# Scores of the 64-feature heads in a two-layer hybrid attention block: three products on half of the rows each, two heads side by side

## The chip, the core and the metric

The kernel runs on one core of one Trainium2 chip. The metric is the device time of one execution in microseconds (us): the median of the runs shown. A core has a matrix engine (TensorE, PE in the profile; PEld is its weight loading, which may overlap the products), a vector engine (DVE), a scalar engine (ACT), GpSimd (POOL), and a queue (SP) that issues the transfers. Products read SBUF, which has 128 partitions (called rows here), and write PSUM banks of 128 x 512 floats.

## The reference

Two layers run over 512 latent tokens and 256 context tokens of width 1024. In each layer one input projection feeds three groups of attention heads, whose outputs go through one output projection, and an MLP of width 4096 follows. Groups A (8 query heads, 2 key heads, a window of 128 with sinks) and B (4 heads, a 2-D neighbourhood with a bias) have 64 features in a head, and the change is about their scores alone:

```python
qa = axial_rope(split_heads(xa_q, A_HEADS), row, col)
ka = axial_rope(split_heads(xa_k, A_KV_HEADS), row, col)
out_a = windowed_gqa(qa, ka, split_heads(xa_v, A_KV_HEADS), ka_c, va_c, attn_sink[l])
out_b = neighbourhood_attention(split_heads(xb_q, B_HEADS), split_heads(xb_k, B_HEADS),
                                split_heads(xb_v, B_HEADS), kb_c, vb_c, na_rpb[l])
# inside both: scores over the local keys and over the 256 context keys, one softmax over both
s_loc = jnp.einsum('bnqkgd,bnskd->bnkgqs', qb, kb) * scale
s_ctx = jnp.einsum('bnqkgd,bckd->bnkgqc', qb, k_ctx) * scale
```

Group C (4 latent heads with 64 + 32 features) is not touched. In the first layer the context tokens attend too, so queries cover 768 tokens there and 512 in the second layer.

## The kernel before

Everything is float32. To keep that precision the kernel splits each operand of a product into a high part that the fast format `float32r` holds and a low part, the rest, and computes high x high + low x high + high x low: three products in place of one. All engines' orders are set by a scheduler at build time, which interleaves independent work; nothing in the kernel text fixes where a product stands among its neighbours.

For each layer the order of the text is: a pair of B heads is projected (`proj_B`), attended (`att_B`), then the second pair, then the keys, values and queries of A (`proj_AK`, `proj_AQ`), the attention of half of A's heads (`att_A`), an output-projection part (`w_out_part`), the rest of A, then group C and the MLP.

A projection (`feat_chunk`, L480 to L482, tile `psd`) gives 128 feature rows: two heads of 64, one on rows 0 to 63 and one on rows 64 to 127. It is copied to `qkraw` (`evac_raw`). Then, for each of the two heads, the kernel lays out operands that fill all 128 rows:

- `stack_q` (L556, L557) writes a page `qs` for each head: the high part of q on the head's own rows, the low part on the other 64 rows.
- `dup_k` (L567 to L576) writes pages `kh` and `kl` for each head: the high part of k on both halves of the rows (the second copy is a transfer inside SBUF, L569), and the low part on both halves (the second copy on DVE, L576).

With them `att_unit` (L617) needs two products of 128 rows for a score: `qs` x `kh` sums high x high and low x high, and `qs` x `kl` adds high x low (and low x low). It works on four "rows" at a time: two heads and two blocks of 128 queries (B), or four heads and one block (A). A row has one or two segments: 256 context keys, and 256 or 384 local keys. A segment has one PSUM bank of the three named `pss`; the vector engine takes it out with the mask and the running minimum (L621 without, L628 with a mask; the scores carry a minus sign), ACT makes the exponentials (L633), DVE, POOL or ACT norms them, TensorE turns the probabilities (L668, tile `pst`) and multiplies them with the values (L682, tile `psv`; two heads side by side on 64 columns each). Group C's scores also run at L617, as three products on 96 rows (tiles `kc`, `qc`).

The pages `qs kh kl vtok bias oth otl` come from one ring of 18 buffers (tag `pg`); `oth` and `otl` hold the attention outputs for the output projection. The weights of a projection arrive in one transfer of 128 columns into a ring of four buffers (`raw`).

One other place matters below: L314 in `ada_dve`, in the MLP of the first layer, turns a small tile with TensorE; in some calls the tile has 64 rows only.

Of the kernel before, what the change touches and what calls it, by code (L numbers as in the profile page):

```python
# [44 lines left out]
        "up": 4, "u": 16, "wf": 16, "of": 8, "fg": 2, "ga": 4}  # L45
# [3 lines left out]
for _tag, _names in (  # L49
# [10 lines left out]
    ("pg", "qs kh kl vtok bias oth otl"),  # L60
# [8 lines left out]
    ("ga", "gate"),  # L69
    ("ac", "acc"),  # L70
# [10 lines left out]
def hybrid_dit_kernel(  # L81
# [13 lines left out]
    def bc(ap):  # L95
        return ap.bitcast(F32)

    def sbuf(n, dt, name):
        tag = TAGS[name]
        size = 768 if tag in PAD else 512 if tag in PAD5 else -(-n // 256) * 256  # L100
        return sb.tile([P, size], dt, tag=tag, name=name, bufs=CAPS[tag])[:, :n]

    def page(n, dt=F32, name="pgf"):
        return sbuf(n, dt, name)

# [445 lines left out]
    def stack_q(t_, n):  # L551

        outs = []
        for own, oth in ((H0, H1), (H1, H0)):
            q_ = page(n, F32R, "qs")
            A.copy(q_[own], t_[own])  # L556
            V.tensor_tensor(q_[oth], t_[own], bc(q_[own]), ALU.subtract)  # L557
            outs.append(q_)
        return outs

    def dup_k(t_, n):

        outs = []
        for own, oth in ((H0, H1), (H1, H0)):
            kh = page(n, F32R, "kh")
            kl = page(n, F32R, "kl")
            A.copy(kh[own], t_[own])  # L567
            if DUPDMA & 1:
                nc.sync.dma_start(bc(kh[oth]), bc(kh[own]))  # L569
            else:  # L570
                A.copy(kh[oth], t_[own])
            V.tensor_tensor(kl[own], t_[own], bc(kh[own]), ALU.subtract)
            if DUPDMA & 2:
                nc.sync.dma_start(bc(kl[oth]), bc(kl[own]))
            else:
                V.tensor_copy(kl[oth], bc(kl[own]))  # L576
            outs.append((kh, kl))
        return outs
# [19 lines left out]
    def att_unit(kind, rows, vap, put, sinkcols=None):  # L598


        pts = []
        for r, row in enumerate(rows):
            w_ = sum(s[1] for s in row["segs"])
            we = w_
            init = HUGE
# [6 lines left out]
            off = 0  # L612
            for c0, n, mask in row["segs"]:
                ps = ps_s()
                np_ = len(row["passes"])
                for j, (lh, rh) in enumerate(row["passes"]):
                    T.matmul(ps[:, :n], lh, rh[:, c0:c0 + n], start=(j == 0), stop=(j == np_ - 1))  # L617
                dst = p_[:, off:off + n]
                acc = small(1, "m", 16)
                if mask is None:  # L620
                    V.tensor_scalar(dst, ps[:, :n], 0.0, init, ALU.add, ALU.min, accum_out=acc)  # L621
                else:
                    src = ps[:, :n]
                    if len(mask.shape) == 3:
                        nb = mask.shape[1]
                        src = src.rearrange("p (b c) -> p b c", b=nb)
                        dst = dst.rearrange("p (b c) -> p b c", b=nb)
                    V.tensor_tensor_reduce(out=dst, in0=src, in1=mask, scale=1.0, scalar=init,  # L628
                                           op0=ALU.add, op1=ALU.min, accum_out=acc)
                init = acc  # L630
                off += n
            sm = small(1, "sm", 16)
            A.activation(p_, p_, AF.Exp, scale=-1.0, bias=init, accum_out=sm)  # L633
            V.reciprocal(sm, sm)  # L634
            e_ = NORM[kind][r]
            if e_ == "V":
                V.tensor_scalar(p_[:, :w_], p_[:, :w_], sm, None, ALU.mult)
            elif e_ == "A":
                A.activation(p_[:, :w_], p_[:, :w_], AF.Copy, scale=sm)
            else:  # L640
                G.tensor_tensor(p_[:, :w_], p_[:, :w_], sm.to_broadcast([P, w_]), ALU.mult)  # L641
            pts.append(p_)
# [99 lines left out]
    for l in range(DEPTH):  # L742
# [11 lines left out]
        def new_ot(c):  # L754
            OT[c] = (page(nq, F32R, "oth"), page(nq, F32R, "otl"))
# [4 lines left out]
        def proj_B(p_):  # L760
# [5 lines left out]
            KB[2 * p_], KB[2 * p_ + 1] = dup_k(t_, 768)  # L766
# [4 lines left out]
            QB[2 * p_], QB[2 * p_ + 1] = stack_q(t_, nq)  # L771
# [4 lines left out]
        def att_B(p_):  # L776
# [13 lines left out]
            for u in range(2 if last else 3):  # L790
                rows = []
                for i in range(2):
                    for n in (2 * u, 2 * u + 1):
                        q_ = QB[2 * p_ + i][:, n * P:(n + 1) * P]
                        kh, kl = KB[2 * p_ + i]
# [10 lines left out]
                        rows.append(dict(passes=[(q_, kh), (q_, kl)], segs=segs))  # L806
# [16 lines left out]
        def proj_AK():  # L823
# [3 lines left out]
            KA.extend(dup_k(t_, 768))  # L827
# [6 lines left out]
        def proj_AQ(jp):  # L834
            for c in (jp, jp + 2):
                res = feat_chunk(l, h, c * P, nq)
                t_ = evac_raw(res, -0.125, False)
                rope(t_, ALLP, (rA[:, 0, :], rA[:, 1, :]), SHUF16)
                QA[2 * c], QA[2 * c + 1] = stack_q(t_, nq)
                pump(1)  # L840
# [476 lines left out]
```

## Time and profile before

| what | value |
| --- | --- |
| median of 3 runs | 1644.02 us (1641.97 to 1644.7) |
| profiled execution, its own time | 1647.55 us |
| its span, first to last instruction | 1645.8 us |
| PE busy | 1594.6 us (97%), 8994 instructions |
| DVE / ACT / POOL busy | 1009.0 / 682.6 / 608.3 us |
| granted TensorE clock, mean | 0.995 of the full 2.4 GHz |
| attention of A and B, first layer | about 60 to 330 us |
| attention of A and B, second layer | about 1000 to 1200 us |

A busy PE is not a PE at its peak: products are pipelined, so the duration of one product (0.28 to 0.39 us here) is longer than the distance from its start to the next one's start, which is what a product costs when they follow each other. The distances are read from the starts in the timeline. In the timeline the form `128*128 128x512` means that weights of 128 rows and 128 columns are in the array and 512 columns are moved through; `64*128` is an array used on 64 rows, `128*64` on 64 columns. Instructions of the same line and tiles that follow each other are printed as one row with their count.

### The profile page before, as it was taken

The numbers are of one execution on the slowest core, as the hardware profiler recorded it, in microseconds if no ns is written. First come the engines' busy times: TensorE is split into PE (matmuls) and PEld (weight loads), VectorE is DVE, ScalarE is ACT, GpSimd is POOL, SyncE is SP. The second block draws the span as 40 slices with busy tenths as digits, with TensorE's granted clock in tenths as the row PEclk, the third lists the DMA queues.
The fourth block names the chain that finished last, engine by engine and source line by source line (L and its number), as shares of the span: only waits on it lengthen the run. The fifth ranks groups of instructions, "written<-read, shape, count | busy, mean of one in ns | idle before, by whom it ended". The sixth has DMA issues, their size and how long they took to land.

```text
span 1645.8 us, 24134 instructions
## 1 busy us (share of the span) xinstructions
PE 1594.6 (97%) x8994; PEld 1361.1 (83%) x8994; DVE 1009.0 (61%) x1995; ACT 682.6 (41%) x1342; POOL 608.3 (37%) x564
## 2 busy tenths in 40 slices
PE   5999999999999999999999999999999999999997
PEld 3888789787898988989989779888777788888886
DVE  3565766687887556454445776786687644334445
ACT  4554466665631312212223145446755522223332
POOL 1111643553433353341533341153453333333335
PEclk9999999999999999999999999999999999999999
DMA  9654311230154333334333722211120233333331
GB/s 318 184 154 127 121 51 28 67 78 1 53 168 132 116 109 115 106 93 136 88 108 99 253 68 76 69 53 51 46 80 14 78 93 98 91 103 103 90 106 73
DMA packets 156421, 164.46 MB, mean 100 GB/s; under 512 B 8960, under 2 KB 111368, under 8 KB 156304
## 3 DMA queue, kind: packets, MB, share of 16 engines
q1 hardware_dynamic: 156304, 162.92, 32.8%
q8 instruction: 71, 1.16, 0.3%
q14 instruction: 46, 0.38, 0.1%
HBM read 155.53 MB, written 2.12 MB: 96 GB/s over the span
## 4 chain that ended last, share of the span: by engine, by line
PE 85%; DVE 7%; DMA 4%; issue 2%; ACT 2%; POOL 0%; SPq 0%; POOLq 0%; DVEq 0%; ACTq 0%
PE psd L1102 8%; PE psd L1103 8%; PE psd L1104 8%; PE pss L617 5%; PE psv L682 5%; PE pst L668 4%; PE psd L480 3%; PE psd L482 3%; PE psd L481 3%; PE pss L1138 3%; PE pss L1136 3%; PE pss L1137 3%; PE psd L720 2%; PE psd L722 2%; PE psd L721 2%
## 5 line engine op out<-in xcount | busy, mean ns | idle before, releaser
L739 POOL TENSOR_TENSOR xlat<-xlat,rtmp 128x512 f32<-128x512 f32 x159 | 235.8, 1506 | 272.3 <-DVE rtmp L738 269.5
L464 DVE TENSOR_TENSOR wl<-raw,wh 128x1024 fp32r<-128x1024 f32 (+1 forms) x168 | 219.0, 1304 | 184.1 <-issue 82.0
L463 ACT CAST wh<-raw 128x1024 fp32r<-128x1024 f32 (+1 forms) x168 | 174.5, 1039 | 297.6 <-PE pst L1138 179.6
L1102 PE MATMUL psd<-hT,wh 128*128 128x384 f32 (+2 forms) x752 | 264.9, 353 | 3.4 <-DVE hT L427 3.4
L1103 PE MATMUL psd<-hT,wl 128*128 128x384 f32 (+2 forms) x752 | 264.3, 351 | 2.3 <-DVE wl L464 2.3
L1104 PE MATMUL psd<-hT,wh 128*128 128x384 f32 (+2 forms) x752 | 265.9, 354 | 0.0
L641 POOL TENSOR_TENSOR prob<-prob,sm 128x512 f32<-128x512 f32 (+3 forms) x110 | 127.6, 1169 | 265.4 <-DVE sm L634 225.1
L1111 POOL TENSOR_TENSOR relu<-relu 128x384 f32<-128x384 f32 (+1 forms) x96 | 96.6, 1008 | 316.6 <-ACT uh L1110 292.4
L1109 ACT ACTIVATE relu<-psd 128x384 f32<-128x384 f32 (+1 forms) x93 | 49.1, 528 | 280.5 <-PE psd L1104 278.1
L633 ACT ACTIVATE prob<-prob,m 128x513 f32<-128x513 f32 (+6 forms) x160 | 120.9, 756 | 100.6 <-DVE m L628 69.0
L1102 PEld LDWEIGHTS psd<-hT,wh 128*128 128x128 f32 x752 | 141.5, 188 | 14.3 <-issue 4.1
L1112 DVE TENSOR_TENSOR ul<-relu,uh 128x384 fp32r<-128x384 f32 (+1 forms) x96 | 60.4, 630 | 150.7 <-POOL relu L1111 150.7
L1103 PEld LDWEIGHTS psd<-hT,wl 128*128 128x128 f32 x752 | 141.5, 188 | 12.5 <-DVE wl L464 3.0
L1104 PEld LDWEIGHTS psd<-hT,wh 128*128 128x128 f32 x752 | 141.5, 188 | 12.3 <-issue 2.5
L287 DVE SCALAR_TENSOR_TENSOR acc<-araw,consts,acc 128x512 f32<-128x512 f32 x140 | 117.7, 867 | 6.6 <-DMA araw<-in_w_ada_dram 5.8
L668 PE MATMUL pst<-consts,prob 128*128 128x128 f32 x688 | 106.1, 277 | 2.2 <-POOL prob L641 1.8
L668 PEld LDWEIGHTS pst<-consts,prob 128*128 128x128 f32 x688 | 79.6, 140 | 29.0 <-issue 17.8
L482 PE MATMUL psd<-hT,wl 128*128 128x384 f32 (+1 forms) x280 | 97.7, 349 | 1.1 <-DVE wl L464 1.1
L480 PE MATMUL psd<-hT,wh 128*128 128x384 f32 (+1 forms) x280 | 97.8, 349 | 0.0
L481 PE MATMUL psd<-hT,wh 128*128 128x384 f32 (+1 forms) x280 | 96.6, 345 | 0.0
L1138 PE MATMUL pss<-wh,ul 128*128 128x512 f32 x224 | 87.3, 390 | 0.0
L1137 PE MATMUL pss<-wl,uh 128*128 128x512 f32 x224 | 87.2, 390 | 0.0
(265 smaller groups left out, 3539.6 us busy)
## 6 DMA issues: line engine op xcount, KB each, us to landing
raw<-in_w_mlp_in_dram SPq DMA_DIRECT2D x64, 512.0 KB
raw<-in_w_mlp_out_dram SPq DMA_DIRECT2D x64, 512.0 KB
araw<-in_w_ada_dram SPq DMA_DIRECT2D x112, 256.0 KB
raw<-in_w_in_dram SPq DMA_DIRECT2D x24, 512.0 KB
raw<-in_w_ada_dram SPq DMA_DIRECT2D x24, 512.0 KB
raw<-in_w_ada_dram SPq DMA_DIRECT2D x32, 256.0 KB
raw<-in_w_out_dram SPq DMA_DIRECT2D x8, 512.0 KB
raw<-in_w_out_dram SPq DMA_DIRECT2D x16, 256.0 KB
```

Source lines behind the costliest of these rows:

```text
L463: A.copy(hi, raw)
L464: V.tensor_tensor(lo, raw, bc(hi), ALU.subtract)
L480: T.matmul(ps[:, :n], wh[:, k, :], hh[k][:, s0:s0 + n], start=(k == 0), stop=False)
L481: T.matmul(ps[:, :n], wh[:, k, :], hl[k][:, s0:s0 + n], start=False, stop=False)
L482: T.matmul(ps[:, :n], wl[:, k, :], hh[k][:, s0:s0 + n], start=False, stop=(k == KC - 1))
L668: T.transpose(pt[:, r * P:(r + 1) * P], pts[r][:, pos[r][kb]:pos[r][kb] + P], ident)
L739: (V if fast and (RLAST if fast == "end" and t == 3 else RFAST)[dh] == "V" else G).tensor_tensor(xt[t][:, cs], xt[t][:, cs], tmp, ALU.add)
L1102: T.matmul(o_, wh[:, k, :], hh[k][:, sl], start=(k == 0), stop=False)
L1103: T.matmul(o_, wl[:, k, :], hh[k][:, sl], start=False, stop=False)
L1104: T.matmul(o_, wh[:, k, :], hl[k][:, sl], start=False, stop=(k == KC - 1))
L1137: T.matmul(a_, uh[:, ts_], wl[:, c % 2, :], start=False, stop=False)
L1138: T.matmul(a_, ul[:, ts_], wh[:, c % 2, :], start=False, stop=fin)
```

## The change

- `stack_q` and `dup_k` go. One function `hi_lo` splits a page of two heads in place: high part on ACT, low part on DVE, each on all 128 rows in one instruction. The pages are `qh`, `ql`, `kh`, `kl`, one of each for two heads. The transfers `kh<-kh` and the copies of `kl` go.
- A score is now three products, `qh` x `kh`, `qh` x `kl`, `ql` x `kh`, each on the 64 rows of its head. Two heads that lie on different halves are written in turn, product by product, into two `pss` banks. The built program gives each of these products a tile of 64 rows and 128 columns, at row 0 or at row 64; before, these products had the full tile of 128 by 128, as have all projections, output projections, turnings and the 96-row products of C.
- The reading of a segment moves into a function `evac_seg` and comes after the products of both heads.
- A query chunk of A now joins head c of the first key group with head c of the second, so its weights come in two transfers of 64 columns (`feat_chunk` takes a pair of columns).
- The output pages leave the ring `pg` for one of their own, `ot`, of 8 double pages.

```diff
-    ("pg", "qs kh kl vtok bias oth otl"),
+    ("pg", "qh ql kh kl vtok bias"),
+    ("ot", "ot"),
...
     def feat_chunk(l, h, c0, ntok):
         hh, hl = h
-        wh, wl = load_split([(ALLP, w3(l, c0, P, 0, KC))], [KC, P], {1280: "w3", 1152: "w4"}.get(c0) if l == 0 else None)
+        src = [(ALLP, w3(l, c0, P, 0, KC))] if isinstance(c0, int) else [
+            ((ALLP, ALLP, slice(64 * i, 64 * i + 64)), w3(l, c_, 64, 0, KC)) for i, c_ in enumerate(c0)]
+        wh, wl = load_split(src, [KC, P], {1280: "w3", 1152: "w4"}.get(c0) if l == 0 else None)
...
-    def stack_q(t_, n):
...
-    def dup_k(t_, n):
...
+    def hi_lo(t_, n, name):
+
+        hi, lo = page(n, F32R, name + "h"), page(n, F32R, name + "l")
+        A.copy(hi, t_)
+        V.tensor_tensor(lo, t_, bc(hi), ALU.subtract)
+        return hi, lo
...
+        pts = [None] * 4
+
+        for rs in ([(0, 2), (1, 3)] if "halves" in rows[0] else [(r,) for r in range(4)]):
+            ps_of = {}
+            if len(rs) == 2:
+                for c0, n, _ in rows[rs[0]]["segs"]:
+                    pss = [ps_s() for _ in rs]
+                    for j in range(3):
+                        for r, ps in zip(rs, pss):
+                            lh, rh = rows[r]["halves"][j]
+                            T.matmul(ps[:, :n], lh, rh[:, c0:c0 + n], start=(j == 0), stop=(j == 2))
+                    for r, ps in zip(rs, pss):
+                        ps_of[r, c0] = ps
+                    for r in rs:
+                        evac_seg(r, rows[r], c0, pts, ps_of, sinkcols)
...
-                        q_ = QB[2 * p_ + i][:, n * P:(n + 1) * P]
-                        kh, kl = KB[2 * p_ + i]
+                        hv = (H0, H1)[i]
+                        (qh, ql), (kh, kl) = [[t_[hv] for t_ in q_] for q_ in (QB[p_], KB[p_])]
+                        qh, ql = qh[:, n * P:(n + 1) * P], ql[:, n * P:(n + 1) * P]
...
-                        rows.append(dict(passes=[(q_, kh), (q_, kl)], segs=segs))
+                        rows.append(dict(halves=[(qh, kh), (qh, kl), (ql, kh)], segs=segs))
...
-            for c in (jp, jp + 2):
-                res = feat_chunk(l, h, c * P, nq)
+            for c in (2 * jp, 2 * jp + 1):
+
+                res = feat_chunk(l, h, (c * 64, 256 + c * 64), nq)
...
-                    q_ = QA[hd][:, n * P:(n + 1) * P]
-                    kh, kl = KA[i // 2]
+                    hv = (H0, H1)[hd // 4]
+                    (qh, ql), (kh, kl) = [[t_[hv] for t_ in q_] for q_ in (QA[hd % 4], KA)]
```

The scheduler places the new products anew. On PE at the first attention unit of the first layer (`hT`, `wh`, `wl` are the operands of a projection; L617 is the score before, L585 turns the values) the order before is:

```order
L482 MATMUL psd<-hT_131,wl 128x384
L617 MATMUL pss<-kh,qs 128x256
L617 MATMUL pss<-kl,qs 128x256
L617 MATMUL pss<-kh,qs 128x256
L617 MATMUL pss<-kl,qs 128x256
L617 MATMUL pss<-kh,qs 128x256
L617 MATMUL pss<-kl,qs 128x256
L585 MATMUL psd<-consts,qkraw 128x128 x6
L617 MATMUL pss<-kh,qs 128x384
L617 MATMUL pss<-kl,qs 128x384
L480 MATMUL psd<-hT_117,wh 128x384
```

The same place of the changed program, with the buffers' numbers (`pss_739` and `pss_740` are the two heads of one pair, `pss_753` and `pss_754` those of the next; L629 is the score, L570 turns the values):

```order
L629 MATMUL pss_739<-kh_640,qh_648 128x256
L629 MATMUL pss_740<-kh_640,qh_648 128x256
L629 MATMUL pss_739<-kl_641,qh_648 128x256
L629 MATMUL pss_740<-kl_641,qh_648 128x256
L629 MATMUL pss_739<-kh_640,ql_649 128x256
L629 MATMUL pss_740<-kh_640,ql_649 128x256
L629 MATMUL pss_753<-kh_640,qh_648 128x256
L629 MATMUL pss_753<-kl_641,qh_648 128x256
L629 MATMUL pss_753<-kh_640,ql_649 128x256
L570 MATMUL psd_714<-consts_66,qkraw_709 128x128 x4
L570 MATMUL psd_720<-consts_66,qkraw_709 128x128 x2
L629 MATMUL pss_754<-kh_640,qh_648 128x256
```

The first pair stands in turn; of the second pair one head's three products follow it, and the other head's three come only after the six turnings of L570, since the ring `pss` has three banks. On PE near the end of A in the second layer (L894 to L896 before, L910 to L912 after, are group C's input projection; L668 and L681 turn probabilities) the order before is:

```order
L894 MATMUL psd<-wh,hT_9466 128x416
L617 MATMUL pss<-kh,qs 128x384
L617 MATMUL pss<-kl,qs 128x384
L895 MATMUL psd<-wl,hT_9466 128x416
L682 MATMUL psv<-pT_ring,vtok 64x256 x8
L668 MATMUL pst<-consts,prob 128x128 x8
```

and in the changed program:

```order
L681 MATMUL pst<-consts,prob 128x128 x6
L629 MATMUL pss<-kh,qh 128x384
L629 MATMUL pss<-kl,qh 128x384
L629 MATMUL pss<-kh,ql 128x384
L910 MATMUL psd<-wh,hT_9541 128x416
L911 MATMUL psd<-wl,hT_9541 128x416
L629 MATMUL pss<-kh,qh 128x256
L629 MATMUL pss<-kl,qh 128x256
L629 MATMUL pss<-kh,ql 128x256
```

Here the three products of one head stand alone between full-tile work, in both programs in small groups among other products. Over the whole program the 432 score products of A and B become 648, which stand in 135 unbroken runs. Outside the two attention stretches the order on PE is the same in both programs.

## Rows read from the trace of the kernel before

**Rows 1.** The page: busy us (share), xinstructions; the chain that ended last.

```profile
PE 1594.6 (97%) x8994; PEld 1361.1 (83%) x8994; DVE 1009.0 (61%) x1995; ACT 682.6 (41%) x1342; POOL 608.3 (37%) x564
...
PE 85%; DVE 7%; DMA 4%; issue 2%; ACT 2%; POOL 0%; SPq 0%; POOLq 0%; DVEq 0%; ACTq 0%
```

**Rows 2.** Stretches: length, busy PE, PEld, DVE, ACT, POOL; clock; DMA share; GB/s.

```profile
60.00:330.00 270.00, 266.38 (x1796) 224.94 (x1796) 176.28 (x511) 146.41 (x344) 95.73 (x126) 1.00 0.34 101
330.00:430.00 100.00, 95.31 (x571) 75.93 (x569) 84.74 (x201) 63.54 (x138) 46.17 (x37) 0.98 0.19 48
1000.00:1200.00 200.00, 196.73 (x1251) 168.54 (x1251) 143.93 (x397) 113.88 (x254) 71.71 (x84) 1.00 0.22 63
1200.00:1290.00 90.00, 82.69 (x497) 65.28 (x496) 74.33 (x167) 55.12 (x109) 40.46 (x32) 0.96 0.25 68
```

**Rows 3.** Two waits of PE, 60 to 330 us: total, times, longest.

```profile
PE psa L222 <- DMA raw<-in_w_ada_dram: 1.2, 1, 1.2
...
PE psd L482 <- DVE wl L464: 0.3, 1, 0.3
```

**Rows 4.** Timeline of PE near 1180 us: start, duration, line, tiles, form.

```profile
1180.15 0.28 PE L617 MATMUL pss<-kl,qs 128*128 128x256 f32 x1
1180.27 0.28 PE L617 MATMUL pss<-kh,qs 128*128 128x256 f32 x1
1180.38 0.28 PE L617 MATMUL pss<-kl,qs 128*128 128x256 f32 x1
1180.50 0.27 PE L668 MATMUL pst<-consts,prob 128*128 128x128 f32 x1
```

**Rows 5.** Timeline of PE near 878 us: 64 rows, then the full tile.

```profile
878.25 0.46 PE L314 MATMUL psd<-consts,arow 64*128 64x64 f32 x4 [0.55 <-DVE arow L311]
878.63 0.44 PE L1102 MATMUL psd<-hT,wh 128*128 128x384 f32 x1
878.91 0.33 PE L1103 MATMUL psd<-hT,wl 128*128 128x384 f32 x1
879.08 0.34 PE L1104 MATMUL psd<-hT,wh 128*128 128x384 f32 x1
```

**Rows 6.** Timeline of PE near 940 us, around two turnings on 64 rows.

```profile
939.88 0.39 PE L1165 MATMUL pss<-wfl,uh 128*128 128x512 f32 x1
940.11 0.39 PE L1166 MATMUL pss<-wfh,ul 128*128 128x512 f32 x1
940.42 0.34 PE L314 MATMUL psd<-consts,arow 64*128 64x64 f32 x2
940.69 0.50 PE L1164 MATMUL pss<-wfh,uh 128*128 128x512 f32 x1
941.03 0.39 PE L1165 MATMUL pss<-wfl,uh 128*128 128x512 f32 x1
```

**Rows 7.** Split of k: line, durations min/median/max in ns, shapes.

```profile
L567 ACT CAST kh<-qkraw x12: 827/831/842, 61.6 to 1073.1; 64x768 fp32r<-64x768 f32 x12
L572 DVE TENSOR_TENSOR kl<-qkraw,kh x12: 937/953/956, 62.5 to 1074.3; 64x768 fp32r<-64x768 f32 x12
L576 DVE CAST kl<-kl x12: 543/554/557, 64.5 to 1076.2; 64x768 fp32r<-64x768 f32 x12
```

**Rows 8.** Timeline of PE near 186 us: modulation, tiles of 32 columns.

```profile
185.94 1.07 PE L222 MATMUL psa<-raw,consts 128*32 128x256 f32 x16
```

**Rows 9.** Timeline of PE's weight loads near 940 us.

```profile
939.88 0.19 PEld L1166 LDWEIGHTS pss<-wfh,ul 128*128 128x128 f32 x1
940.42 0.20 PEld L314 LDWEIGHTS psd<-consts,arow 64*128 64x128 f32 x2 [0.35 <-issue]
```

**Rows 10.** Line L314, 870 to 980 us: durations min/median/max in ns.

```profile
L314 PE MATMUL psd<-consts,arow x8: 220/223/272, 878.2 to 974.9; 64*128 64x64 f32 x8
```

**Rows 11.** Timeline of PE near 366 us: turnings, group C's products.

```profile
365.75 1.04 PE L668 MATMUL pst<-consts,prob 128*128 128x128 f32 x8
366.54 0.60 PE L617 MATMUL pss<-kc,qc 96*128 96x256 f32 x3
```

More of the change, by code (lines that the diff above doesn't have):

```diff
@@ L596, in evac_copy, with evac_seg @@
             V.tensor_copy(dst, src)
[L598 to L605, printed above, removed]
+    def evac_seg(r, row, c0, pts, ps_of, sinkcols):
+        w_ = sum(s[1] for s in row["segs"])
+        off = 0
+        for c_, n, mask in row["segs"]:
+            if c_ == c0:
+                break
+            off += n
+        if off == 0:
+            we, init = w_, HUGE
             if sinkcols is not None:
@@ L632, in att_unit @@
[L632 to L641, printed above, removed]
@@ new lines, in evac_seg, with att_unit @@
+        pts[r] = (p_, acc, w_)
+    def att_unit(kind, rows, vap, put, sinkcols=None):
+        pts = [None] * 4
[12 more added lines that the diff above has]
+                        evac_seg(r, rows[r], c0, pts, ps_of, sinkcols)
+            else:
+                row = rows[rs[0]]
+                for c0, n, _ in row["segs"]:
+                    ps = ps_s()
+                    np_ = len(row["passes"])
+                    for j, (lh, rh) in enumerate(row["passes"]):
+                        T.matmul(ps[:, :n], lh, rh[:, c0:c0 + n], start=(j == 0), stop=(j == np_ - 1))
+                    ps_of[rs[0], c0] = ps
+                    evac_seg(rs[0], row, c0, pts, ps_of, sinkcols)
+            for r in rs:
+                p_, init, w_ = pts[r]
+                sm = small(1, "sm", 16)
+                A.activation(p_, p_, AF.Exp, scale=-1.0, bias=init, accum_out=sm)
+                V.reciprocal(sm, sm)
+                e_ = NORM[kind][r]
+                if e_ == "V":
+                    V.tensor_scalar(p_[:, :w_], p_[:, :w_], sm, None, ALU.mult)
+                elif e_ == "A":
+                    A.activation(p_[:, :w_], p_[:, :w_], AF.Copy, scale=sm)
+                else:
+                    G.tensor_tensor(p_[:, :w_], p_[:, :w_], sm.to_broadcast([P, w_]), ALU.mult)
+                pts[r] = p_
@@ L754, in new_ot @@
         def new_ot(c):
-            OT[c] = (page(nq, F32R, "oth"), page(nq, F32R, "otl"))
+            OT[c] = page2(nq, "ot")
         QB, KB, VB = {}, {}, {}
@@ L856, in att_A @@
                         segs.append((b0 * P, (b1 - b0 + 1) * P, maskA[:, m0:m0 + b1 - b0 + 1, :]))
-                    rows.append(dict(passes=[(q_, kh), (q_, kl)], segs=segs))
+                    rows.append(dict(halves=[(qh, kh), (qh, kl), (ql, kh)], segs=segs))
                 def put(pv, n=n, jp=jp):
```

74 lines of the change are left out of this document (25 added, 49 removed).

## Prediction

> **What bounds the kernel now.** I read the page first, for the share of each engine, then the busy time by stretch, the waits of PE in the stretches that the change touches, and last the timeline of PE at single products. The page shows a PE that is busy 97% of the span, and a chain of work that is PE for 85% of it [rows 1]; no other engine is above 61%. A busy PE could still be loosely packed, so the stretches matter more: where A and B are attended, PE is idle for 270 - 266.4 = 3.6 us in the first layer and 200 - 196.7 = 3.3 us in the second, at the full granted clock [rows 2]. One wait in the first of them, for a transfer of the modulation's weights, is 1.2 us of it [rows 3]. So there is almost nothing to win here from DVE, ACT or transfers, and a change in what PE must do goes into the time one for one, less at most these 7 us.
>
> **What a score product costs now.** Starts tell it: L617 starts at 1180.15, 1180.27, 1180.38 and the next work at 1180.50 [rows 4], so a product of 256 columns costs 0.12 us. Products of 384 columns stand 0.17 apart (878.91 to 879.08) [rows 5], those of 512 columns 0.23 (939.88 to 940.11) [rows 6]. That is 256, 384 and 512 columns at 2.4 per ns and 13 ns more, so I use 0.119 and 0.173. The full tile of 128 rows is common to the scores and to all that stands around them, turnings and projections alike, so nothing is paid for passing from one to the other.
>
> **What the change takes away beside PE.** The split of q and k halves its instructions, and their duration hangs on the elements in a row, not on the rows. ACT loses 6 of 12 `kh` of 0.83 us and 12 of 24 `qs` of the same kind, at most as long, 15 us; DVE loses 6 `kl` of 0.95, 12 copies of 0.55 and 12 `qs`, again at most 0.95, some 24 us; 12 transfers inside SBUF go [rows 7]. All this lies beside PE's work. It can give back only PE's idle time, 7 us in the two stretches [rows 2], and not all of that, since a part waits for transfers. I take 3 us; the ends are 0 and 7. The 8 weight loads of A's queries become 16 transfers of half the size; PE waited 0.3 us for weights of a projection [rows 3], the ring of four buffers being ahead, so I take nothing. If that cover failed, each could cost as much as the longest wait on a transfer in the stretch, 1.2 us, some 10 us. The new ring for the outputs only loosens waits; the same 7 us bound it.
>
> **What PE's products cost after.** Before there are 336 products of 256 columns and 96 of 384: 336 x 0.119 + 96 x 0.173 = 56.6 us. Afterwards there are 504 and 144, which one after another would take 84.9 us (+28.3). If every product ran beside its partner on the other half, it would be half, 42.4 us (-14.2). The built order decides between these. In it two products on different halves stand next to each other, free to overlap, less often than the kernel text has them: going through the 135 runs, with a product waiting only for the one before it on its own half, 134 products (105 of 256 columns, 29 of 384) begin while the other half still works. 399 x 0.119 + 115 x 0.173 = 67.4 us remain, **+10.8 us**. That two products on different rows do overlap is not in the trace. The nearest row is that of the modulation's products, which sit on different columns, 32 each: 16 of 256 columns are through in 1.07 us [rows 8], where 256 columns at 2.4 per ns one after another make 1.7; so parts of the array do work side by side. I take overlap, and keep +28.3 as the other end.
>
> **What the change of tile costs.** This is the largest term, and the diff doesn't show it. The trace before has 64-row tiles in three places, L314. Around 940 us the last 512-column product starts at 940.11; the next in the same tile would start at 940.34. The 64-row one starts at 940.42 [rows 6], **0.09 us** late, and its weights are loaded only then, after 0.35 us in which the loader waited for nothing but its turn [rows 9]; a 512-column neighbour's weights are loaded during the product before it. Its second product follows more slowly than the others of its kind: 272 ns against a median of 223 [rows 10], 0.05 us, since the load was not hidden. Way back: the second L314 starts at 940.42 + 0.34 - 0.22 = 940.54 and L1164 at 940.69, 0.15 later; four of the kind at 878 us take 0.46 together [rows 5], which without the last one's 0.22 and the first one's 0.05 leaves 0.06 for each step; again 0.09. And that first full product takes 0.50 instead of 0.39, and the next starts 0.34 after it instead of 0.23 [rows 6]: 0.11 for a load that nothing hid. At 878 us it is the same, 0.28 to the next instead of 0.17 [rows 5].
>
> So a way in and out of the 64-row tile costs 0.09 + 0.11 going in (a load of 128 columns is exposed, as in L1164) and 0.09 + 0.11 coming out, or 0.09 + 0.05 where turnings follow. The built order has 135 runs of new products: 132 are entered from full tiles (3 from another narrow tile, where a change was due anyway), 99 end before full products, 30 before turnings, 6 before value products, which change the tile in any case. 132 x 0.20 + 99 x 0.20 + 30 x 0.14 = 26.4 + 19.8 + 4.2 = **50 us**. Before, the scores cost no change at all. The other narrow tiles change about as often as before. A run that starts where PE waited anyway hides its way in, but there are only 7 us of such waiting.
>
> The Trainium skill, TensorEngine Tiling (Array Packing), Key Properties, says that a change of tiling mode, not merely of the tile, drains TensorE. The trace agrees with 0.09 us each way. The page gives no price; it is the rule that speaks against this change; without a drain the sum would be that of rival (c) below.
>
> **The sum.** 10.8 + 50 - 3 = +58 us on the profiled execution's 1647.55, so 1705.5; it stands 3.5 us above the median of the runs, which makes 1702. Readers of banks are late next: no run of the new order holds more than three segments, the number of `pss` banks, but 27 runs hold all three and need them free at once. I take nothing, as full products stand between; half a microsecond (one reading by DVE) for each would be 13 us.
>
> **The rivals.**
> (a) *Halves do not overlap*: loads of 128 columns for both halves go one after the other, and the weights set the pace. For it: nothing in the trace runs on two row halves at once. Then the products cost +28.3: 1702 + 17.5 = 1720.
> (b) *Half of the tile changes are hidden*: the scheduler often puts a run where PE would have waited, or the load is pulled ahead within the engine. Against it: both places of L314 read above show the whole price. 1702 - 25 = 1677.
> (c) *The other side, not slower*: 64 rows change no tile for PE, as the 96-row products of group C, on the full tile, change none: after eight turnings from 365.75 the first of them starts at 366.54, 0.02 after the last turning [rows 11]. Place: the 132 ways in and out; price nothing instead of 0.38 us a run. Then 10.8 remain, the freed DVE and ACT take back all of the 7 us, and the output pages' own ring takes some of the 4.7 + 7.3 us that PE idles in C's stretches [rows 2]: 1644, no change. It decides from below 0.03 us for a run. The rows of the 64-row tiles speak against it [rows 5, 6, 9].
> (d) *The pairs give their full half and the tile is free*: -14.2 us, 1630. The order doesn't have the pairs, so this is what the change says but not what the program does. The Trainium skill, the same page, Theoretical Speedup, has up to 2x for products of at most 64 rows; no run here shows it yet.
>
> **How the numbers follow.** Chances: forecast 0.60 (1690 to 1715), (a) 0.19, (b) 0.10, (c) 0.06, (d) 0.02, and 0.03 for longer still by waits for banks. The likeliest is 1702. The range that leaves out 2 in 10 goes from (b), 1676, past (a) with a few us of bank waits, to 1726. A measurement of this kernel can tell 0.2%, 3.3 us, from no change. Slower by more than that are the forecast, (a), (b) and the longer case, 0.92; (c) gives 0.05 to no change and 0.01 to faster; (d) makes faster 0.03.
>
> **What would show it.** In the profile after: the stretches outside attention keep their length, and the first stretch grows by some 32 us, the second by some 26 (the first has 74 of the 135 runs and 60 of the 108 pairs of segments). A score's first product starts about 0.09 us later than its neighbour's pace allows, its load begins with it, with 0.3 us or so of idle loader before, and the first product behind a run is 0.11 us longer. Two products on different halves start some 7 ns apart if they overlap, 0.12 if (a) holds. DVE's busy time falls by some 24 us at most, ACT's by 15, and PE's own waits do not grow. The prediction is wrong if the first product of a run starts at the ordinary distance with its weights loaded ahead, or if the time is lost in waits of PE for `pss` banks or weights.

## The result

The changed kernel takes **1692.21 us** (median of 4 runs, 1691.42 to 1693.04) against 1644.17 for the kernel before beside it: **1.0285 times as long**, 95% interval 1.0263 to 1.0307. That is slower by 48 us; forecast were 1702 and a range of 1676 to 1726. The profiled execution has a span of 1690.5 us, 44.7 longer than before.

The page of the changed kernel (busy us and share of the span, then the chain that ended last), against [rows 1]:

```profile
PE 1649.5 (98%) x9210; PEld 1366.1 (81%) x9210; DVE 990.9 (59%) x1965; ACT 671.4 (40%) x1324; POOL 609.5 (36%) x564
...
PE 88%; DVE 6%; DMA 3%; issue 2%; ACT 1%; SPq 0%; POOL 0%; POOLq 0%; DVEq 0%; ACTq 0%
```

PE is busy 54.9 us longer; the other engines have less to do or the same. PE's idle time, span less busy, fell from 51.2 to 41.0 us. Two attention stretches of the changed kernel (length, busy PE, PEld, DVE, ACT, POOL, clock, DMA share, GB/s), against [rows 2]:

```profile
60.00:330.00 270.00, 269.73 (x1778) 208.26 (x1778) 154.67 (x465) 128.85 (x309) 80.78 (x109) 1.00 0.32 93
1040.00:1240.00 200.00, 199.64 (x1213) 152.03 (x1211) 123.82 (x346) 101.64 (x227) 65.79 (x80) 1.00 0.18 50
```

Of 3.6 and 3.3 us of idle PE, 0.3 and 0.4 are left, at the full granted clock. The time is therefore not lost in waits; PE itself has more to do. Where, the first products of the two MLPs tell, which stand behind the attention of each layer. By line, before and then after: durations in ns, first and last start in us.

```profile
L1102 PE MATMUL psd<-hT,wh x752: 278/334/522, 425.4 to 1593.0; 128*128 128x384 f32 x124, 128*128 128x512 f32 x59, 128*128 128x256 f32 x5
...
L1102 PEld LDWEIGHTS psd<-hT,wh x256: 186/188/192, 1280.0 to 1592.7; 128*128 128x128 f32 x128
```

```profile
L1118 PE MATMUL psd<-hT,wh x752: 274/334/522, 450.1 to 1637.8; 128*128 128x384 f32 x124, 128*128 128x512 f32 x59, 128*128 128x256 f32 x5
...
L1118 PEld LDWEIGHTS psd<-hT,wh x256: 186/188/193, 1324.9 to 1637.6; 128*128 128x128 f32 x128
```

The first MLP begins 24.7 us later (425.4 to 450.1), the second another 20.2 (1280.0 to 1324.9), and from there to the end nothing is added (1645.8 - 1280.0 = 365.8; 1690.5 - 1324.9 = 365.6). All of it is in the two attention stretches.

**One run of new scores.** The timeline of PE at the first run of the changed kernel (start, duration, line, tiles, form, how many), and its weight loads:

```profile
69.55 0.34 PE L488 MATMUL psd<-hT,wh 128*128 128x384 f32 x1
69.72 0.33 PE L489 MATMUL psd<-hT,wl 128*128 128x384 f32 x1
69.98 0.39 PE L629 MATMUL pss<-kh,qh 64*128 64x256 f32 x2
70.21 0.28 PE L629 MATMUL pss<-kl,qh 64*128 64x256 f32 x2
70.33 0.28 PE L629 MATMUL pss<-kh,ql 64*128 64x256 f32 x2
70.44 0.28 PE L629 MATMUL pss<-kh,qh 64*128 64x256 f32 x1
70.56 0.28 PE L629 MATMUL pss<-kl,qh 64*128 64x256 f32 x1
70.68 0.28 PE L629 MATMUL pss<-kh,ql 64*128 64x256 f32 x1
70.89 0.55 PE L570 MATMUL psd<-consts,qkraw 128*128 128x128 f32 x3
```

```profile
69.55 0.19 PEld L489 LDWEIGHTS psd<-hT,wl 128*128 128x128 f32 x1
69.98 0.19 PEld L629 LDWEIGHTS pss<-kh,qh 64*128 64x128 f32 x2 [0.25 <-issue]
```

Read four things here. A full product of 384 columns is followed after 0.17; the first score starts 0.26 after it, 0.09 late. Its weights are loaded at 69.98, together with it, and the loader sat idle for 0.25 before, with nothing to wait for but its turn. The second pair then starts 0.22 after the first in place of 0.12: 0.10 for a load that nothing hid. Behind the run, the turnings start 0.21 after the last score, 0.09 late again. And the pairs do overlap: each row of "x2" holds two products of the two halves, which start 3 ns apart and take no longer together than one. The run of nine products has gained three starts of 0.12 by that, and paid 0.09 + 0.10 going in and 0.09 + 0.06 coming out.

The whole line in the changed kernel, durations min/median/max and what its engine (PE's loader too) sat idle for (us, times), shows the same 100 times over. "Issue" is time in which the loader waited for nothing that the profile shows; for the score line of the kernel before it is 1.2 us, 3 times.

```profile
L629 PEld LDWEIGHTS pss<-kh,qh x216: 182/183/189, 70.0 to 1230.0; 64*128 64x128 f32 x108
...
  issue: 22.6, 100
```

**The account.** I went through all runs of scores of A and B in both traces, product by product: how far each start lies behind the one before it, beyond that one's own pace (columns / 2.4 + 13 ns for a product on all columns, 109 ns for a turning). In us:

| | before, 146 runs | after, 135 runs | difference | forecast |
| --- | --- | --- | --- | --- |
| first score late | -1.8 | 14.8 | +16.6 | |
| first load not hidden | 5.3 | 12.7 | +7.4 | |
| first work behind the run late | 2.8 | 13.3 | +10.5 | |
| its load not hidden | 0.0 | 13.3 | +13.3 | |
| **tile changes together** | 6.3 | 54.1 | **+47.8** | +50 |
| **the products themselves** | 58.3 | 61.5 | **+3.2** | +10.8 |

The first two rows of "before" belong together: behind turnings, which is where 54 of those runs stand, the first score starts 0.08 us ahead of the turnings' pace and the next one as much late.

The sum is +51.0, but the table reads one thing twice. Nine runs of the changed kernel follow the run before them with a single product in between, and that product's unhidden load stands in the last row of the one run and in the first row of the next: 1.7 us, against -0.3 in the kernel before. Counted once, the tile changes are **+45.8** and the sum is +49.0. Three more runs of value products (70 against 67, 0.42 each, as worked out in an experiment below) add 1.3. From a layer's first score to its MLP (length, busy PE, PEld, DVE, ACT, POOL, clock, DMA share, GB/s), before and then after:

```profile
69.30:425.40 356.10, 347.91 (x2285) 288.09 (x2283) 250.79 (x697) 202.23 (x467) 139.13 (x160) 1.00 0.28 82
1005.40:1280.00 274.60, 266.72 (x1663) 222.02 (x1663) 203.42 (x540) 158.93 (x346) 107.58 (x110) 0.99 0.21 57
```

```profile
70.00:450.10 380.10, 375.32 (x2405) 289.41 (x2405) 245.03 (x686) 196.49 (x460) 140.18 (x161) 1.00 0.26 74
1028.10:1324.90 296.80, 291.71 (x1759) 225.24 (x1759) 199.55 (x529) 156.28 (x339) 107.03 (x110) 0.99 0.18 49
```

PE's idle time in them, length less busy, fell from 16.1 to 9.9 us, by 6.2, of which 2.2 lay inside the runs and is in the table already: -4.0. That makes +46.3, and the two stretches grew by 46.2 (630.7 to 676.9). Outside of them the changed kernel is 1.5 us shorter: 0.7 longer up to the first score, 2.0 shorter between the first MLP's start and the second layer's first score, 0.2 shorter at the end.

### The profile page after: what moved, and what is told of

Read it like the earlier page. It is cut to its first block, busy times and chain, and to the rows that moved or that the text cites. A ratio compares the mean times of both kernels' runs of the same rounds, so it can differ in the third digit from the quotient of the medians.

```text
span 1690.5 us, 24493 instructions
## 1 busy us (share of the span) xinstructions
PE 1649.5 (98%) x9210; PEld 1366.1 (81%) x9210; DVE 990.9 (59%) x1965; ACT 671.4 (40%) x1324; POOL 609.5 (36%) x564
## 4 chain that ended last, share of the span: by engine, by line
PE 88%; DVE 6%; DMA 3%; issue 2%; ACT 1%; SPq 0%; POOL 0%; POOLq 0%; DVEq 0%; ACTq 0%
PE psd L1118 8%; PE psd L1119 8%; PE psd L1120 8%; PE pss L629 5%; PE psv L695 5%; PE pst L681 5%; PE psd L487 3%; PE psd L489 3%; PE psd L488 3%; PE pss L1153 3%; PE pss L1154 3%; PE pss L1152 3%; PE psd L733 2%; PE psd L734 2%; PE psd L735 2%
## 5 line engine op out<-in xcount | busy, mean ns | idle before, releaser
L681 PE MATMUL pst<-consts,prob 128*128 128x128 f32 x688 | 108.2, 280 | 1.3 <-POOL prob L654 1.0
L681 PEld LDWEIGHTS pst<-consts,prob 128*128 128x128 f32 x688 | 78.1, 140 | 33.2 <-issue 21.2
L489 PE MATMUL psd<-hT,wl 128*128 128x384 f32 (+1 forms) x280 | 98.7, 352 | 1.1 <-DVE wl L469 1.1
L686 ACT COPY pT_ring<-pst 128x512 f32<-128x512 f32 x124 | 70.6, 585 | 65.6 <-PE pst L681 63.5
```

Of the source, the lines that this page charges most:

```text
L489: T.matmul(ps[:, :n], wl[:, k, :], hh[k][:, s0:s0 + n], start=False, stop=(k == KC - 1))
L681: T.transpose(pt[:, r * P:(r + 1) * P], pts[r][:, pos[r][kb]:pos[r][kb] + P], ident)
```

## The experiments

Theories to be told apart: T, the tile changes cost about 0.38 us a run and make up nearly all of it; (a), the halves do not overlap; (b), half of the tile changes are hidden; (c), the tile costs nothing, and the time comes from the third product or from something else that the change moved. Rival (d), a faster kernel, is out by the result.

| run | what | us | ratio to before, 95% |
| --- | --- | --- | --- |
| changed kernel | | 1692.21 | 1.0263 to 1.0307 |
| e1_full3 | three products, full tile | 1670.80 | 1.0143 to 1.0177 |
| e2_full2 | two products, full tile, new split | 1636.08 | 0.9944 to 0.9973 |
| e3_one_half | both heads on one half | 1715.89 | 1.0430 to 1.0466 |
| e4_before64 | kernel before, 64 rows | 1691.40 | 1.0273 to 1.0307 |
| e5_rows96 | kernel before, 96 rows | 1643.70 | 0.9976 to 1.0007 |
| e6_more_runs | changed kernel, 161 runs | 1701.47 | 1.0319 to 1.0369 |
| e7_grouped | changed kernel, heads one behind the other | 1693.38 | 1.0272 to 1.0305 |
| f1_vals6_raw3 | kernel before, longer runs of values | 1662.47 | 1.0083 to 1.0126 |
| f2_vals6_w4 | the same, other ring smaller | 1659.25 | 1.0072 to 1.0116 |
| f3_copies | kernel before, one copy by transfer | 1649.51 | 1.0023 to 1.0053 |

The median of the kernel before was 1643.30 beside e1 to e4, 1644.60 beside e5, e6, f1 and f2, and 1644.37 beside e7 and f3.

### The tile alone, taken away and put in

Three products as in the changed kernel, in the same 135 runs, but on all 128 rows (in A likewise):

```diff
-                        (qh, ql), (kh, kl) = [[t_[hv] for t_ in q_] for q_ in (QB[p_], KB[p_])]
+                        (qh, ql), (kh, kl) = QB[p_], KB[p_]
```

> The changed kernel with its three products for each score on the full tile of 128 rows: each operand is the whole page, so a score is the sum over both heads of a page and the output is not the reference's. The order on TensorE is the changed kernel's own, 135 runs at the same places, without a change of tile. Theory (the time lies in the 135 ways into and out of the 64-row tile, some 0.39 us each, and 64-row products of two heads overlap): the ways, 53 us, go, and the overlap goes too, so 648 products cost 84.9 us in place of about 60: 1692 - 53 + 24 = 1663 us. Rival (the time lies in a third more products and weight loads, or in waits for the three score banks that a pair takes two of): all of that is still here, so 1692 or a little more.

Measured: 1670.80. With half as many products again in full length, and no overlap at all, the kernel is 21 us faster than the changed one. (c) is out, and so is (b): had only half of the tile's price been paid, the changed kernel would be slower than this one by no more than 10.8 + 25 - 28.3 = 8 us. PE at the end of a run and the beginning of the next in it:

```profile
71.65 0.28 PE L629 MATMUL pss<-kh,ql 128*128 128x256 f32 x1
71.77 0.82 PE L570 MATMUL psd<-consts,qkraw 128*128 128x128 f32 x6
```

The turnings follow 0.12 behind the last score, where it was 0.21 on the half tile. The forecast of 1663 was 8 us short. In the profiled run (span 23.6 longer than before) the two attention stretches, from the first score to the first MLP and from the end of that MLP to the second, are longer by 12.4 and 7.0, together the 19 that were expected; 4.2 more lie outside of them, in work that no edit touches: 1.4 ahead of the first score, 1.1 in the first MLP, 1.6 from the start of the second MLP on. The granted clock was lower in this execution at all three: 0.88 of 2.4 GHz up to the first score (0.98 in the kernel before), 0.66 in the ten us from 436, around the start of the first MLP, where PE waits for 3.0 (0.83 at the same place before, from 422, with the same wait), and 0.66 in the ten us from 1304, just into the second MLP, with PE idle for 1.4 (1.00 from 1282 before). A clock of 0.66 there means 6.8 of the ten us at 1.2 GHz and the rest at 2.4. So these 4.2 are likely the clock's in the main, not the edit's.

The other way round, the kernel before with its two products on rows 0 to 63 and nothing else changed in its text (the scheduler makes 149 runs of scores of it, where the kernel before has 146):

```diff
-                    T.matmul(ps[:, :n], lh, rh[:, c0:c0 + n], start=(j == 0), stop=(j == np_ - 1))
+                    hf = slice(0, 64) if kind in "AB" else slice(None)
+                    T.matmul(ps[:, :n], lh[hf], rh[hf, c0:c0 + n], start=(j == 0), stop=(j == np_ - 1))
```

> The kernel before with its two products for each score of groups A and B on rows 0 to 63 alone (the other 64 rows are left out of the sum). As many products, of as many columns, as before; the built order has 149 runs of them, each now in a 64-row tile, always at row 0. Theory (a way into and out of the 64-row tile costs about 0.39 us): 149 x 0.39 = 58 us, less some 6 us of idle time: 1696 us. Rival (a narrow tile costs nothing by itself; the changed kernel loses by its pairs, its third product or its waits): 1644 us.

Measured: 1691.40. No third product, no new split, no new transfers, no new rings: the tile alone costs 48 us. PE at its first run:

```profile
71.35 0.33 PE L482 MATMUL psd<-hT,wl 128*128 128x384 f32 x1
71.61 0.38 PE L618 MATMUL pss<-kh,qs 64*128 64x256 f32 x1
71.83 0.28 PE L618 MATMUL pss<-kl,qs 64*128 64x256 f32 x1
71.95 0.28 PE L618 MATMUL pss<-kh,qs 64*128 64x256 f32 x1
```

It is the picture of the changed kernel: 0.26 to the first score, 0.22 to the second, 0.12 from then on. Over its 149 runs the account gives 115.9 us for the scores, where the kernel before has 64.6 (the two lines in bold): 51.3 more, or 49.0 when the loads between two runs are counted once.

Fewer rows are not enough, as the same edit with 96 rows shows:

```diff
-                    hf = slice(0, 64) if kind in "AB" else slice(None)
+                    hf = slice(0, 96) if kind in "AB" else slice(None)
```

> The kernel before with its two products on rows 0 to 95 of the 128 (the last 32 of each sum over 128 left out, so the scores are not the reference's); the instructions stand in the same order as in the kernel before, and the same 146 runs of scores. It leaves fewer rows busy, as the half-row products do, but not on a row half. Theory (it is the change to the tile of 64 rows that costs, not that part of the array is idle): 1644, within 0.3% of the kernel before, and the first score of a run starts 0 us late. Rival (any product on fewer rows than its neighbours stops the queue, or lets the load be late): 146 runs x 0.35 = +51, so about 1693, as with 64 rows.

Measured: 1643.70, ratio 0.9992. Its first scores start on time (-1.7 us over 146 runs, against -1.8 before). The built program gives these 96-row products the full tile of 128 by 128, in the kernel before's own order. It is leaving the full tile that costs, not leaving rows of it unused.

### More runs of the same products

> The changed kernel, nothing left out, with the pairs of score products given an earlier place in the queue, so that its scores stand in 161 runs in place of 135, with the same 648 products. Theory (the price goes by the runs, about 0.39 us for each entry, exit and exposed load): 26 x 0.39 = +10, so 1702 (1699 to 1706). Rival (the price goes by the products or by the bytes, both unchanged): 1692, within 3.

```diff
+                    with tc.high_priority(offset=40):
                         for j in range(3):
```

Measured: 1701.47, 9.3 above the changed kernel for 26 runs, 0.36 each. The same work in more pieces costs more, as T has it. Not all of it is the tile: by the account, counted once, the ways in and out cost 6.8 us more, and the products themselves 3.1, since in smaller pieces 157 of them start beside another in place of 180.

### Overlap

Both heads of a pair on rows 0 to 63 (the second one's scores come from the features of the first):

```diff
-                        hv = (H0, H1)[i]
+                        hv = H0
```

> The changed kernel with both heads of a pair taken from rows 0 to 63, so the second head of each pair is computed from the first one's data. Tiles of 64 rows, 135 runs and their places are the changed kernel's, but no two products can lie on different halves. Theory (products on different halves overlap, also where three of one head follow three of the other in the program): all 648 products come one after another, 84.9 in place of some 60 us: 1692 + 24 = 1716 us. If only products that alternate in the program overlap: 1692 + 17 = 1709. Rival (halves do not overlap, loads set the pace): 1692.

Measured: 1715.89. The ways in and out cost the same as in the changed kernel (14.8, 12.7 and 13.1 us by the account), and the runs themselves 98.7 in place of 74.2. So the overlap of the halves is worth 24.5 us in the changed kernel. This is rival (a) built; the prediction gave 1720 for it.

That overlap was larger than the forecast, so I put the three products of a head one behind the other, which leaves less of it if starts keep the program's order:

```diff
-                    for j in range(3):
-                        for r, ps in zip(rs, pss):
+                    for r, ps in zip(rs, pss):
+                        for j in range(3):
```

> The changed kernel, nothing left out, with the three products of a head one behind the other in the program, first those of rows 0 to 63, then those of rows 64 to 127, in place of rows in turn; 137 runs of scores against 135 (+0.8). In the trace of the changed kernel some products on one row half start ahead of products on the other half that stand before them in the program. Theory (each row half keeps an order of its own, and a product on the other half may go first): the halves overlap nearly as before, the products of a run cost 60 to 65, so 1693 to 1698. Rival (starts keep the program's order, and only a product of one half beside the next of the other overlaps): one start in three can be beside another in place of one in two; by the stretch per run with both heads on one half, +24.5 with no overlap, some two thirds of that are lost, +13 to +16, so 1706 to 1709.

Measured: 1693.38, the same as the changed kernel within 1.2. In the built program of this kernel the first run reads, in order: `kh,qh`, `kl,qh`, `kh,ql` of the first head, then the same three of the second, then three of the next pair's first head. The timeline of PE there:

```profile
68.19 0.33 PE L489 MATMUL psd<-hT,wl 128*128 128x384 f32 x1
68.45 0.39 PE L629 MATMUL pss<-kh,qh 64*128 64x256 f32 x2
68.67 0.29 PE L629 MATMUL pss<-kl,qh 64*128 64x256 f32 x2
68.79 0.29 PE L629 MATMUL pss<-kh,ql 64*128 64x256 f32 x2
68.91 0.28 PE L629 MATMUL pss<-kh,qh 64*128 64x256 f32 x1
69.03 0.28 PE L629 MATMUL pss<-kl,qh 64*128 64x256 f32 x1
```

The two `kh,qh` start together at 68.45 (10 ns apart), though the second stands fourth in the program, behind the `kl,qh` and `kh,ql` that start at 68.67 and 68.79. The halves work off their products side by side, each in its own order. Added up over the built order with each half kept to its own order alone, the products of this kernel come to 62.4 us; with starts in the program's order they would come to 71.9. The trace has 63.0.

### The cheaper split alone

The changed kernel with the full tile and only two products, low q x high k left out (the `j` loop ends at 2):

> As the full-tile version of the changed kernel, with two products for each score (the third, low q by high k, is left out, and heads are summed). TensorE then does as much as in the kernel before, and what is left of the change is the cheaper split on ACT and DVE, the transfers that went, the own ring of the output pages and the two heads read after each other. Theory (all that lies beside TensorE, which idles 7 us in the stretches of A and B before): 1637 to 1644 us. Rival (the split and the transfers were on the path): clearly below 1637. Rival (reading banks in pairs costs time): above 1645.

Measured: 1636.08, 7 us below the kernel before and 1 below the range that was expected. Everything that the change brings beside its products is worth this much: half the instructions of the split, fewer transfers, the outputs' own ring, and the runs that came out of it (121). PE's busy time is 6.2 us less than before and its idle time 5.6 less in the profiled runs (11.8 by the profiles, as the profiled execution before was a long one), so this is probably in part a better order, not only shorter waits; the two were not taken apart.

### Trying for a version that beats both

The kernel before has tile changes too, around the value products (columns in halves). By the same account its 67 runs of them cost 10.4 us on entry (some 3 of it waits for operands), 13.2 on exit and 4.4 behind it. Six blocks of keys in a row make fewer of them:

```diff
-PVB = 3
-NPT = 4
+PVB = 6
+NPT = 6
```

with a smaller ring elsewhere to make room, once of raw weights, once of `w4`.

> The kernel before, nothing left out and scores as before, with the turnings and value products of six blocks of keys in a row in place of three (a ring of six turned blocks in place of four; for its room the ring of raw weights has three places in place of four). Value products stand in 43 runs in place of 67. In the trace of the kernel before the runs of value products cost 10.4 us on entry, 13.2 on exit and 4.4 behind it, 28.0 for 67, 0.42 each. Theory (tile changes cost whoever makes them): 24 x 0.42 = -10, so 1634 (1630 to 1639). Rival (the first value product then waits longer for turned blocks, or weights come later, and it is spent again): 1644 or above.

> As the run with the ring of raw weights at three places, with six blocks of keys in a row, but the room is taken from another ring (four in place of five places of split weights of the layer's second projection; raw weights keep four places). Value products in 44 runs in place of 67. Theory: 23 x 0.42 = -10, so 1634 (1630 to 1640), and the same as the other within 3, if the smaller ring matters in neither. Rival: 1644 or above; a difference between the two of over 4 would put a cost on one of the two rings.

Measured: 1662.47 and 1659.25, both slower by 15 to 18 us. The page of the second one:

```profile
span 1655.5 us, 24142 instructions
...
PE 1590.2 (96%) x8994; PEld 1361.6 (82%) x8994; DVE 1025.4 (62%) x1995; ACT 689.3 (42%) x1342; POOL 615.5 (37%) x564
```

What PE and its loader sat idle for ahead of value products (L682; us, times), in it:

```profile
  ACT pT_ring L673: 14.3, 20
  issue: 3.8, 17
```

and in the kernel before:

```profile
  issue: 10.0, 38
...
  ACT pT_ring L673: 1.3, 5
```

The runs are fewer, and PE's busy time is 4.4 us less in this version, as meant (the ways in and out fell from 28.0 to 23.2); in the first version it is 1.6 more. But PE's idle time rose from 51.2 to 1655.5 - 1590.2 = 65.3, by 14.1. The value products wait for ACT to copy the last turned blocks out of PSUM: 14.3 us in place of 1.3, most of it idle time of the loader ("issue", 3.8 in place of 10.0, is the tile change again, with fewer runs). What PE itself waited for, of this and of weights that ACT splits (total, times, longest):

```profile
PE psv L682 <- ACT pT_ring L673: 5.2, 7, 1.8
...
PE psd L1102 <- ACT wh L463: 1.5, 3, 0.7
PE psd L480 <- ACT wh L463: 1.3, 2, 0.7
...
PE pss L1136 <- ACT wh L463: 1.0, 1, 1.0
```

The kernel before has none of these four waits. They are 9.0 of the 14.1 us; the rest is spread over smaller ones. So the rival had it right, in this version in both of its halves: turned blocks come late, and so do weights. That three blocks in a row let other work run in between and six do not is the likely reason; the order was not taken apart further. The two rings differ by 3 us, so neither matters much.

> The kernel before, nothing left out, with the second copy of the low half of k made by a transfer too, in place of a VectorE copy (the first copy of the high half is already made so). Leaving out the low q with the whole of k's doubling took 8 us from the kernel before, while TensorE's idle in the two stretches with such scores is 4.7 and 7.3. Theory (VectorE's copies behind the split hold these scores up, in part): 1638 to 1642. Rival (the copies lie beside other work, the gain there was from the products and runs that moved): 1644, within 3; a third (the transfers arrive later than the copies did): 1647 or above.

```diff
-DUPDMA = 1
+DUPDMA = 3
```

Measured: 1649.51, slower by 5. DVE is 6.5 us less busy (1002.5) and nothing is won by it. That is the third expectation's range, but its reason doesn't show: PE waits 0.3 us for these transfers. The profiled span is only 1.8 longer, since the profiled execution before stood 3.5 us above its median and this one stands at it; of the 5, three more runs of value products (70) would be 1.3. The rest isn't explained. No version found beats the kernel before, other than by leaving work out.

## Why the prediction was right, and where it was not

**Direction and cause: right.** PE was the bound and its added work went into the time. The tile changes are the largest term, measured directly by e4 (48 us for 149 runs).

**Tile changes: +50 forecast, +45.8 found** (counted once). The single prices read from L314 [rows 5, 6, 9] hold: 0.09 late going in (median 0.094), 0.10 for the first load, 0.09 coming out (median 0.087), 0.11 for the full product behind and 0.056 for a turning. The forecast took the scores before as free of such costs; the table has 6.3 us for them. That is no price of their own tile: nearly all of it is waits, and the ends of those runs that touch the narrow tiles of the modulation and of the value products. About a tenth of the ways in cost 0.17 to 0.26 in place of 0.09: these stand behind a single full product between two runs, whose own load stands open, behind a single full product that had started early behind turnings, or behind the modulation's narrow tiles. The drain that the Trainium skill names (TensorEngine Tiling (Array Packing), Key Properties) fits both ways; e5 shows no such price where the mode stays.

**Products: +10.8 forecast, +3.2 found. This is the step that failed.** The prediction says that a product waits only for the one before it on its own half, but its count of 134 overlapped products also let no product start ahead of one that stands before it in the program, on either half. With both rules the built order comes to 66 us (67.4 in the prediction), with the first alone to 61.0, and 61.5 is measured. In the trace 180 of the 648 start less than half a pace behind the one before, and e7 shows why: each half keeps only its own order. At 71.69 in the changed kernel, where in the program the three products of `pss_754` stand ahead of three of the next pair on the other half, both first ones have started before the second of either:

```profile
71.69 0.58 PE L629 MATMUL pss<-kh,qh 64*128 64x256 f32 x2
71.92 0.28 PE L629 MATMUL pss<-kl,qh 64*128 64x256 f32 x1
72.03 0.28 PE L629 MATMUL pss<-kh,ql 64*128 64x256 f32 x1
72.11 0.28 PE L629 MATMUL pss<-kl,qh 64*128 64x256 f32 x1
72.23 0.27 PE L629 MATMUL pss<-kh,ql 64*128 64x256 f32 x1
72.49 0.44 PE L487 MATMUL psd<-hT,wh 128*128 128x384 f32 x1
```

Six products take 0.54 from first start to last (72.23 - 71.69); one after another it would be 5 x 0.12 and the 0.10 of the first load, 0.70. The Trainium skill, TensorE: Matmul & The Clock Gate, Part 3, The mechanism, says that products start and end strictly in the program's order. This trace shows otherwise for products on different row halves: in e7 the fourth starts 0.21 us ahead of the second.

**Give-back: -3 forecast, -6.2 found in the two stretches** (2.2 of it stands in the table, in the rows of the scores). The prediction set 7 us as the end for A and B alone and took less than half, holding that waits for transfers would stay. A PE that needs longer for the same stretch is late for all of them; so the whole of the idle there was the better estimate. The other 4.0 of the 10.2 by which PE's idle time fell are mostly not the change's. At the first transfers and at one wait at L294, in the MLP of the first layer, PE idled 15.3 and 2.6 us before, and 13.8 and 0.6 after; e5, which runs in the order of the kernel before, has 13.8 and 0.7.

**From the profile to the median.** The forecast subtracted 3.5 us, as the profiled execution before stood that far above its median. The one after stands at its median (1692.25 and 1692.21). So the subtraction was right, and the difference is 44.7 by the profiles and 48.0 by the medians. Where the surplus of the execution before lies, e5 shows, whose profiled execution stands at its median (1643.58 and 1643.70): it is 1.4 us shorter up to the first score (67.9 against 69.3), 1.9 at the wait just named, and 1.3 in the second layer's attention.

**Smaller steps.** The split costs by the elements in a row, not by the rows: `kl` took 0.953 on 64 rows [rows 7] and takes 0.956 on 128.

```profile
L562 DVE TENSOR_TENSOR kl<-qkraw,kh x6: 940/956/959, 63.3 to 1088.6; 128x768 fp32r<-128x768 f32 x6
```

DVE fell by 18.1 us (24 at most forecast) and ACT by 11.2 (15). The first layer's attention grew by 24.0 us (32 forecast), the second's by 22.2 (26), both short by the products and the give-back. Waits for `pss` banks, for which some us were left in the range, did not come: PE's idle in these stretches is 0.3 and 0.4 us.

## What to carry to other kernels

Price a smaller tile by the unbroken runs in which its products stand in the built order, not by the products: here a run cost about 0.34 to 0.40 us, 0.20 going in and 0.14 to 0.20 coming out. A pair of heads saves 4 x 0.12 - 3 x 0.12 = 0.12 a segment when perfectly overlapped, so a run needs three full pairs to pay for its ends, and three PSUM banks hold one and a half. Where a scheduler spreads small groups among full-tile work, fill the tile instead, and before making runs longer, look at who has to feed them.

## What was not expected of the hardware

Products on the two row halves of TensorE start out of the program's order, each half in its own: in e7 a product that stands three places later starts 10 ns behind the first and 0.21 us ahead of the second, and the kernel with heads one behind the other is as fast as the one with heads in turn (1693.4 and 1692.2 us). Loads of 128 columns for both halves go on side by side as well: a load takes 0.18 us, and in a run a pair with its two loads takes 0.12.
